# Scores of the first 128 keys in float32r halves, one tile later, in a hybrid gMLP and retention encoder step

## The chip, the cores and the metric

The kernel runs on one core of one Trainium2 chip. The metric is device time in microseconds, the median of several executions. The times before are 2776.47, 2776.78 and 2777.16 us.

## The reference

A two-layer encoder step on 256 prompt frames and 32 sample frames (288 columns in all) with a model width of 2048. Layer 0 mixes tokens by spatial gating, layer 1 by retention; each is followed by a SwiGLU feed-forward layer, and each part by a layer norm of `ALPHA * x + part(x)`. The change lies in the retention of layer 1, with 8 heads of 256 key and 512 value dimensions:

```python
def retention_block(q, k, v, s0, decay, inner, zeta, blk_decay):
    scores = jnp.einsum('bhqd,bhkd->bhqk', q, k) * decay[None]
    intra = jnp.einsum('bhqk,bhkv->bhqv', scores, v)
    cross = jnp.einsum('bhqd,bhdv->bhqv', q, s0) * inner[None, :, :, None]
    s_new = blk_decay[None, :, None, None] * s0 + jnp.einsum(
        'bhkd,bhkv->bhdv', k * zeta[None, :, :, None], v)
    return intra + cross, s_new
...
    proj = x @ w_in
    q, k, v, g = jnp.split(proj, [RET_QK, 2 * RET_QK, 2 * RET_QK + RET_V], axis=-1)
    ...
    q = rope(heads(q, RET_DK), pos) * (RET_DK ** -0.5)
    k = rope(heads(k, RET_DK), pos)
    ...
    o = (o - mu) * lax.rsqrt(var + GN_EPS)
    y = (jax.nn.silu(g.astype(jnp.float32)) * o).astype(x.dtype) @ w_out
```

All arithmetic of the reference is float32. The outputs are the encoded frames, the retention states after prompt and sample, and some rows of the gating layer.

## The kernel before

Activations lie with features on the partitions and the 288 frames as columns. A projection is a sequence of 128x128 weight blocks; a **tile** is one 128-row output, 16 blocks deep here. Precision comes from halves: `split` writes the rounded value as float32r (a cast on ACT) and the rest as a second float32r tile (a subtraction on DVE). A block then takes three float32r matmuls (weight high by x high, weight high by x low, weight low by x high; lines 106 to 108). The weights stream from HBM in chunks of eight blocks; `prep` loads chunk c + 3 and splits it into `whi` and `wlo` when chunk c begins, with three raw and four split buffers. Where the frames are 288 columns the matmul's access pattern is reordered in groups of four columns (`turned`); `fourth` does the same for the other float32r products (`mm4`, line 179).

PE runs in program order. The order of ACT, DVE and POOL is set at build time by a scheduler; each then runs its list in order. What follows a tile is put at a place in the program with `core.after(n, fn)`: `tick` is called at the end of each tile and runs what has come due.

In `retention`, the output columns come head by head: heads 0 and 1 with four gate tiles ahead of values, keys and queries; then values, keys and queries of heads 2 and 3, then both heads' gates, then half of the output projection; the same for heads 4 to 7, with the gates of 4 and 5 behind each head's queries. For each head:

- `turn` (line 705) rotates keys or queries (`rope`, six DVE operations, tiles `rk` and `rq` in the trace) when both their tiles are there. Keys go through `k_move` by a transpose and DRAM into row layout (`k_room`, `kw`), and `k_split` (line 741) makes their decayed halves, `self.wait` ticks later. Queries schedule `scores` after `self.wait` ticks. That is 3 for head 0 and 2 for the others.
- `scores` (line 761) makes three sets of float32 products into one PSUM bank: the first 128 keys by all 256 prompt queries (line 766), the second 128 keys by the second 128 queries (line 768), and the sample's keys, copied three times to 96 rows (line 713), by the sample's queries (line 770). DVE multiplies by the decay table, and the results are split for the next products.
- `v_move` and `v_split` bring the values into row layout (`v_room`, `vw`, `vz`) and split them into `vv`.
- `attend` (line 802) comes one tick after keys, values and scores are all there: products with state and values (`os`, `ss`, `ob`, `sp`), the new states written out, then `normalise` and `o_move`, which transposes the output back through DRAM (`o_room`, `of`), and `o_gate` three ticks later.

All these DRAM transfers are issued on POOL's queue. Most tiles of the stage have a single buffer.

Of the kernel before, what the change touches and what calls it, by code (L numbers as in the profile page):

```python
# [10 lines left out]
F32 = mybir.dt.float32  # L11
F32R = mybir.dt.float32r
I32 = mybir.dt.int32
AF = mybir.ActivationFunctionType
ALU = mybir.AluOpType
# [4 lines left out]
P = 128  # L20
D = 2048
KT = D // P
NP = 256
NS = 32
NT = NP + NS
# [3 lines left out]
NR = 3 * NS  # L29
# [146 lines left out]
def fourth(nc):  # L176

    def mm(out, w, x, **kw):
        nc.tensor.matmul(turned(out, 4), w, turned(x, 4), **kw)

    return mm
# [267 lines left out]
def split(nc, hi, lo, f):  # L449
    nc.scalar.copy(hi, f)  # L450
    nc.vector.tensor_tensor(lo, f, hi.bitcast(F32), ALU.subtract)  # L451
# [176 lines left out]
def retention(core, cst, x, y, lnp, prev, ins, st_p_out, st_s_out):  # L628
    tc, nc = core.tc, core.nc
    xh, xl = x  # L630
    xs = lambda k: (xh[:, k, :NT], xl[:, k, :NT])
    mm, mm4 = nc.tensor.matmul, fourth(nc)
    with ExitStack() as es:
        pool = es.enter_context(tc.tile_pool(name="ret", bufs=1, reuse_waits="tile"))
# [10 lines left out]
        nc.gpsimd.dma_start(inn, ins["inner"])  # L645
        ln = PostNorm(core, cst, x, y, lnp, 2)
        pss = pool.tile([P, 2 * NS], F32R, tag="pss", name="r_ps")
        zero = pool.tile([P, NS], F32, name="r_zero")
        nc.gpsimd.memset(zero, 0.0)
        nc.scalar.copy(pss[:NR, NS:], zero[:NR, :])  # L650
        heads = {}
# [7 lines left out]
            return t[:, :4 * NT].rearrange("p (b i s) -> p b i s", b=9, i=4)  # L659

        def rope(dst, a, b, cos, sin, nm):
            t1 = pool.tile([P, NT], F32, tag="rt1", name=f"rt1{nm}", bufs=1)
            t2 = pool.tile([P, NT], F32, tag="rt2", name=f"rt2{nm}", bufs=1)
            nc.vector.tensor_tensor(t1, a[:, :NT], cos, ALU.mult)
            nc.vector.tensor_tensor(t2, b[:, :NT], sin, ALU.mult)
            nc.vector.tensor_tensor(dst[:, 0, :NT], t1, t2, ALU.subtract)
            nc.vector.tensor_tensor(t1, a[:, :NT], sin, ALU.mult)
            nc.vector.tensor_tensor(t2, b[:, :NT], cos, ALU.mult)
            nc.vector.tensor_tensor(dst[:, 1, :NT], t1, t2, ALU.add)

        class Head:
            def __init__(self, h):
                self.h = h
                self.wait = 3 if h == 0 else 2
                self.ps = {}
                self.left = {"k", "v", "s"}
                self.open = {"o", "g"}
                self.dec = pool.tile([P, NT], F32, tag="dec", name=f"dec{h}")
                nc.gpsimd.dma_start(self.dec, ins["decay"][h])
                self.sg = pool.tile([P, 4, NT], F32, tag="rsg", name=f"rsg{h}", bufs=2)  # L680

            def evac(self, m, ps):
                h = self.h
                if m < 32:
                    self.ps[m % 2] = ps
                    if m % 2:
                        turn = lambda p=dict(self.ps): self.turn(m, p)
                        if h == 0:
                            core.after(2, turn)
                        else:  # L690
                            turn()
                elif m < 64:
                    i = m % 4
                    if i == 0:
                        self.tv = blocks(f"tv{h}", h)
                    nc.vector.transpose(self.tv[:, :, i, :], ps[:, :NT])
                    if i == 3:
                        self.v_move()
                else:
                    i = m % 4  # L700
                    nc.scalar.activation(self.sg[:, i, :], ps[:, :NT], AF.Silu)
                    if i == 3:
                        core.after(1, lambda: self.o_gate("g"))

            def turn(self, m, ps):
                h = self.h
                isk = m >= 16
                nm = ("k" if isk else "q") + str(h)
                r = pool.tile([P, 2, NP + (NR if isk else NS)], F32, tag="kr" if isk else "qr", name="r" + nm)
                rope(r, ps[0], ps[1], cs[:, 0, :], cs[:, 1, :], nm)  # L710
                if isk:
                    self.kr = r
                    nc.scalar.copy(r[:, :, NT:].rearrange("p d (r n) -> p d r n", r=2),
                                   r[:, :, NP:NT].unsqueeze(2).broadcast_to([P, 2, 2, NS]))
                    self.k_move()
                else:
                    self.qr = r
                    qf = pool.tile([P, 2, NS], F32, tag="qf", name=f"qf{h}")
                    qi = pool.tile([P, 160], F32R, tag="qi", name=f"qi{h}")
                    self.qi = qi[:, 20:20 + 4 * NS].rearrange("p (d a n) -> p d a n", d=2, a=2)  # L720
                    nc.vector.tensor_tensor(qf, r[:, :, NP:], inn[:, h, :].unsqueeze(1).broadcast_to([P, 2, NS]), ALU.mult)
                    split(nc, self.qi[:, :, 0, :], self.qi[:, :, 1, :], qf)
                    core.after(self.wait, self.scores)

            def proceed(self, what, i=3):
# [35 lines left out]
            def scores(self):  # L761
                h = self.h
                self.proceed("s")
                b = core.bank(f"sc{h}")
                for d in range(2):
                    mm(b[:, 0:NP], self.kr[:, d, 0:P], self.qr[:, d, 0:NP], start=d == 0, stop=d == 1)
                for d in range(2):
                    mm(b[:, NP:NP + P], self.kr[:, d, P:NP], self.qr[:, d, P:NP], start=d == 0, stop=d == 1)
                for d in range(2):
                    mm(b[:NR, 384:384 + NS], self.kr[:, d, NP:], self.qr[:, d, NP:], start=d == 0, stop=d == 1)  # L770
                pf = pool.tile([P, 384], F32, tag="pf", name=f"pf{h}")
                self.ph = pool.tile([P, 384], F32R, tag="ph", name=f"ph{h}")
                self.pl = pool.tile([P, 384], F32R, tag="pl", name=f"pl{h}")
                psf = pool.tile([P, NS], F32, tag="psf", name=f"psf{h}")
                nc.vector.tensor_tensor(pf[:, :NP], b[:, :NP], self.dec[:, :NP], ALU.mult)
                nc.vector.tensor_tensor(pf[:, NP:], b[:, NP:384], self.dec[:, :P], ALU.mult)
                nc.vector.tensor_tensor(psf[:NR, :], b[:NR, 384:384 + NS], self.dec[:NR, NP:], ALU.mult)
                r = slice(2 * NS, NR)
                nc.scalar.copy(pss[:NR, :NS], psf[:NR, :])
                nc.vector.tensor_tensor(pss[r, :NS], psf[r, :], pss[r, :NS].bitcast(F32), ALU.subtract)  # L780
                split(nc, self.ph, self.pl, pf)

            def v_move(self):
                h = self.h
# [135 lines left out]
        for grp in range(2):  # L920
            a, b, c, d = order[4 * grp:4 * grp + 4]
# [12 lines left out]
def hybrid_step(ctx, tc, ins, outs):  # L934
# [34 lines left out]
    ln = gmlp(core, cst, x, y, lnp, ins, outs["v"], lambda s: load(s + 4))  # L969
    ln = ffn(core, cst, x, y, lnp, 0, ln)  # L970
    ln = retention(core, cst, x, y, lnp, ln, ins, outs["st_p"], outs["st_s"])
    ffn(core, cst, x, y, lnp, 1, ln, outs["yT"])
    core.flush()
# [86 lines left out]
```

## Time and profile before

| what | value |
|---|---|
| median of the runs | 2776.78 us |
| profiled execution | 2779.29 us, its span 2777.5 us |
| granted TensorE clock | 0.999 |
| PE, DVE, ACT, POOL busy | 100%, 60%, 45%, 5% |
| retention stage | from about 1114 to 1862 us of the span |

The profile shows one execution. Busy time of PE counts each matmul with its fill and drain, so neighbouring matmuls overlap in it; the chain of waits counts from start to start. An idle engine that is not the bound costs nothing. In the trace a float32 matmul of the source stands as two rows, since it is run in two passes.

### The profile page before, as it was taken

To read this page: it belongs to the slowest core of one execution; us is meant where nothing else is said; L and a number is where in the kernel's file an instruction comes from. 1 tells how busy PE (TensorE), PEld (TensorE's weight loads), DVE (VectorE), ACT (ScalarE), POOL (GpSimd) and SP (SyncE) were. 2 spreads that over 40 slices of the span, in tenths; PEclk is the share of its full clock that TensorE was granted. 3 is DMA by queue.
4 is the path that set the end of the run, shared out by engine and by line. 5 is a ranking of instruction groups with operands and counts; after the bars stand their busy time and mean duration, and the time that the engine had idled before them with its cause. 6 is when DMAs were issued, how large, how long until landed. Compare 5 with 4: busy or idle time off the path is not lost.

```text
span 2777.5 us, 51381 instructions
## 1 busy us (share of the span) xinstructions
PE 2764.5 (100%) x21574; PEld 2750.9 (99%) x21574; DVE 1665.4 (60%) x2358; ACT 1241.7 (45%) x1645; POOL 141.3 (5%) x241
## 2 busy tenths in 40 slices
PE   9999999999999999999999999999999999999998
PEld 9999999999999999999999999999999999999998
DVE  5688854445444466767765666767844445444465
ACT  5465643433334344644543444445633433333343
POOL 1100000000000000012200111200000000000001
PEclk9999999999999999999999999999999999999999
DMA  7655455555555555567765666755555555555553
GB/s 270 217 189 166 166 178 175 172 172 174 175 175 175 172 175 178 189 205 236 230 198 173 200 216 214 232 194 175 168 174 174 175 174 173 172 173 175 175 174 126
DMA packets 147672, 515.49 MB, mean 186 GB/s; under 512 B 18080, under 2 KB 22448, under 8 KB 147408
## 3 DMA queue, kind: packets, MB, share of 16 engines
q1 hardware_dynamic: 133072, 473.47, 51.1%
q0 software_dynamic: 14224, 38.59, 4.7%
q8 instruction: 168, 2.75, 0.4%
q14 instruction: 64, 0.52, 0.0%
q10 hardware_dynamic: 144, 0.15, 0.0%
HBM read 486.98 MB, written 25.17 MB: 184 GB/s over the span
## 4 chain that ended last, share of the span: by engine, by line
PE 98%; DVE 1%; DMA 1%; issue 0%; ACT 0%; POOL 0%; SPq 0%; DVEq 0%; POOLq 0%
PE af_in L107 13%; PE af_in L108 13%; PE af_in L106 13%; PE ab_in L106 7%; PE ab_in L107 7%; PE ab_in L108 7%; PE af_out L106 6%; PE af_out L107 6%; PE af_out L108 6%; PE ab_out L107 2%; PE ab_out L106 2%; PE ab_out L108 2%; PE aa_in L108 2%; PE aa_in L106 2%; PE aa_in L107 2%; PE aa_out L106 1%
## 5 line engine op out<-in xcount | busy, mean ns | idle before, releaser
L451 DVE TENSOR_TENSOR wlo<-raw,whi 128x1024 fp32r<-128x1024 f32 (+1 forms) x892 | 1086.0, 1218 | 883.6 <-ACT whi L450 879.4
L450 ACT CAST whi<-raw 128x1024 fp32r<-128x1024 f32 (+1 forms) x892 | 933.1, 1047 | 1382.8 <-issue 336.5
L107 PE MATMUL af_in<-xl,whi 128*128 128x288 f32 (+1 forms) x2816 | 812.6, 289 | 0.0
L106 PE MATMUL af_in<-xh,whi 128*128 128x288 f32 (+1 forms) x2816 | 812.3, 288 | 0.0
L108 PE MATMUL af_in<-xh,wlo 128*128 128x288 f32 (+1 forms) x2816 | 812.3, 288 | 0.0
L108 PEld LDWEIGHTS af_in<-xh,wlo 128*128 128x128 f32 x2816 | 527.7, 187 | 0.0
L107 PEld LDWEIGHTS af_in<-xl,whi 128*128 128x128 f32 x2816 | 527.7, 187 | 0.0
L106 PEld LDWEIGHTS af_in<-xh,whi 128*128 128x128 f32 x2816 | 527.7, 187 | 0.0
L106 PE MATMUL ab_in<-xh,whi 128*128 128x288 f32 (+1 forms) x1536 | 443.9, 289 | 0.0
L107 PE MATMUL ab_in<-xl,whi 128*128 128x288 f32 (+1 forms) x1536 | 443.3, 289 | 0.0
L108 PE MATMUL ab_in<-xh,wlo 128*128 128x288 f32 (+1 forms) x1536 | 443.2, 289 | 0.0
L108 PE MATMUL af_out<-hh,wlo 128*128 128x288 f32 x1408 | 405.9, 288 | 0.0
L106 PE MATMUL af_out<-hh,whi 128*128 128x288 f32 x1408 | 405.9, 288 | 0.0
L107 PE MATMUL af_out<-hl,whi 128*128 128x288 f32 x1408 | 405.9, 288 | 0.0
L107 PEld LDWEIGHTS ab_in<-xl,whi 128*128 128x128 f32 x1536 | 287.9, 187 | 0.3
L106 PEld LDWEIGHTS ab_in<-xh,whi 128*128 128x128 f32 x1536 | 287.9, 187 | 0.3
L108 PEld LDWEIGHTS ab_in<-xh,wlo 128*128 128x128 f32 x1536 | 287.9, 187 | 0.0
L107 PEld LDWEIGHTS af_out<-hl,whi 128*128 128x128 f32 x1408 | 263.8, 187 | 0.0
L108 PEld LDWEIGHTS af_out<-hh,wlo 128*128 128x128 f32 x1408 | 263.8, 187 | 0.0
L106 PEld LDWEIGHTS af_out<-hh,whi 128*128 128x128 f32 x1408 | 263.8, 187 | 0.0
L108 PE MATMUL aa_in<-xh,wlo 128*128 128x288 f32 x512 | 148.4, 290 | 1.2 <-DVE wlo L451 1.2
L106 PE MATMUL aa_in<-xh,whi 128*128 128x288 f32 x512 | 148.7, 290 | 0.1
(240 smaller groups left out, 2867.0 us busy)
## 6 DMA issues: line engine op xcount, KB each, us to landing
raw<-in_wpack_dram SPq DMA_DIRECT2D x887, 512.0 KB, 3.3
v_room<-tv POOLq DMA_DIRECT2D x32, 144.0 KB, 5.0
of<-o_room POOLq DMA_DIRECT2D x32, 144.0 KB, 5.3
vw<-v_room POOLq DMA_DIRECT2D x8, 512.0 KB, 5.3
out_st_s_dram<-sso POOLq DMA_DIRECT2D x16, 256.0 KB, 2.6
out_st_p_dram<-so POOLq DMA_DIRECT2D x16, 256.0 KB, 2.9
o_room<-to POOLq DMA_DIRECT2D x8, 512.0 KB, 3.8
y<-in_xT_dram SPq DMA_DIRECT2D x8, 288.0 KB, 5.5
```

Source lines behind the costliest of these rows:

```text
L106: mm(ps, hi, xh, start=first, stop=False)
L107: mm(ps, hi, xl, start=False, stop=False)
L108: mm(ps, lo, xh, start=False, stop=last)
L450: nc.scalar.copy(hi, f)
L451: nc.vector.tensor_tensor(lo, f, hi.bitcast(F32), ALU.subtract)
```

## The change

The product of the first 128 keys with the 256 prompt queries is no longer two float32 matmuls but six float32r matmuls on split keys and queries. `turn` makes the halves (`qa`, `qb`, `ka`, `kb`). The sample's keys are no longer copied to 96 rows: their product has 32 rows, and the decayed sample scores are copied into the three row groups afterwards. The decayed scores are split in two pieces (256 and 128 columns). Every head waits 3 ticks, for `scores` and for `k_split` alike. Scratch tiles (`rt1`, `rt2`, `qf`, `pf`, `psf`, the zero tile) come from the norm's six shared temporary buffers (`prev.tmp`) rather than from own ones.

```diff
-        zero = pool.tile([P, NS], F32, name="r_zero")
+        zero = prev.tmp("r_zero")[:, :NS]
...
-            t1 = pool.tile([P, NT], F32, tag="rt1", name=f"rt1{nm}", bufs=1)
-            t2 = pool.tile([P, NT], F32, tag="rt2", name=f"rt2{nm}", bufs=1)
+            t1 = prev.tmp(f"rt1{nm}")
+            t2 = prev.tmp(f"rt2{nm}")
...
-                self.wait = 3 if h == 0 else 2
+                self.wait = 3
...
-                r = pool.tile([P, 2, NP + (NR if isk else NS)], F32, tag="kr" if isk else "qr", name="r" + nm)
+                r = pool.tile([P, 2, NT], F32, tag="kr" if isk else "qr", name="r" + nm)
+                parts = [pool.tile([P, 2, P if isk else NP], F32R, tag=nm[0] + x, name=nm + x) for x in "ab"]
                 rope(r, ps[0], ps[1], cs[:, 0, :], cs[:, 1, :], nm)
                 if isk:
                     self.kr = r
-                    nc.scalar.copy(r[:, :, NT:].rearrange("p d (r n) -> p d r n", r=2),
-                                   r[:, :, NP:NT].unsqueeze(2).broadcast_to([P, 2, 2, NS]))
                     self.k_move()
+                    self.kp = parts
+                    split(nc, *parts, r[:, :, :P])
                 else:
...
+                    self.qp = parts
+                    split(nc, *parts, r[:, :, :NP])
                     core.after(self.wait, self.scores)
...
-                for d in range(2):
-                    mm(b[:, 0:NP], self.kr[:, d, 0:P], self.qr[:, d, 0:NP], start=d == 0, stop=d == 1)
+                (kh, kl), (qh, ql) = self.kp, self.qp
+                prods = [(l[:, d, :], r[:, d, :]) for d in range(2) for l, r in ((kh, qh), (kh, ql), (kl, qh))]
+                for i, (l, r) in enumerate(prods):
+                    mm4(b[:, 0:NP], l, r, start=i == 0, stop=i == len(prods) - 1)
...
-                    mm(b[:NR, 384:384 + NS], self.kr[:, d, NP:], self.qr[:, d, NP:], start=d == 0, stop=d == 1)
-                pf = pool.tile([P, 384], F32, tag="pf", name=f"pf{h}")
+                    mm(b[:NS, 384:384 + NS], self.kr[:, d, NP:], self.qr[:, d, NP:], start=d == 0, stop=d == 1)
+                pf = [prev.tmp(f"pf{h}{i}") for i in range(2)]
...
-                nc.vector.tensor_tensor(psf[:NR, :], b[:NR, 384:384 + NS], self.dec[:NR, NP:], ALU.mult)
-                r = slice(2 * NS, NR)
-                nc.scalar.copy(pss[:NR, :NS], psf[:NR, :])
-                nc.vector.tensor_tensor(pss[r, :NS], psf[r, :], pss[r, :NS].bitcast(F32), ALU.subtract)
-                split(nc, self.ph, self.pl, pf)
+                nc.vector.tensor_tensor(psf[:NS, :], b[:NS, 384:384 + NS], self.dec[:NS, NP:], ALU.mult)
+                for r in range(2):
+                    nc.scalar.copy(pss[r * NS:(r + 1) * NS, :NS], psf[:NS, :])
+                nc.vector.tensor_tensor(pss[2 * NS:NR, :NS], psf[:NS, :], pss[:NS, :NS].bitcast(F32), ALU.subtract)
+                split(nc, self.ph[:, :NP], self.pl[:, :NP], pf[0][:, :NP])
+                split(nc, self.ph[:, NP:], self.pl[:, NP:], pf[1][:, :P])
```

More of the change, by code (lines that the diff above doesn't have):

```diff
@@ L712, in turn @@
                     self.kr = r
-                    nc.scalar.copy(r[:, :, NT:].rearrange("p d (r n) -> p d r n", r=2),
-                                   r[:, :, NP:NT].unsqueeze(2).broadcast_to([P, 2, 2, NS]))
                     self.k_move()
+                    self.kp = parts
+                    split(nc, *parts, r[:, :, :P])
                 else:
                     self.qr = r
-                    qf = pool.tile([P, 2, NS], F32, tag="qf", name=f"qf{h}")
+                    qf = prev.tmp(f"qf{h}")[:, :2 * NS].rearrange("p (d n) -> p d n", d=2)
                     qi = pool.tile([P, 160], F32R, tag="qi", name=f"qi{h}")
@@ L769, in scores @@
                 for d in range(2):
-                    mm(b[:NR, 384:384 + NS], self.kr[:, d, NP:], self.qr[:, d, NP:], start=d == 0, stop=d == 1)
-                pf = pool.tile([P, 384], F32, tag="pf", name=f"pf{h}")
+                    mm(b[:NS, 384:384 + NS], self.kr[:, d, NP:], self.qr[:, d, NP:], start=d == 0, stop=d == 1)
+                pf = [prev.tmp(f"pf{h}{i}") for i in range(2)]
                 self.ph = pool.tile([P, 384], F32R, tag="ph", name=f"ph{h}")
                 self.pl = pool.tile([P, 384], F32R, tag="pl", name=f"pl{h}")
-                psf = pool.tile([P, NS], F32, tag="psf", name=f"psf{h}")
-                nc.vector.tensor_tensor(pf[:, :NP], b[:, :NP], self.dec[:, :NP], ALU.mult)
-                nc.vector.tensor_tensor(pf[:, NP:], b[:, NP:384], self.dec[:, :P], ALU.mult)
-                nc.vector.tensor_tensor(psf[:NR, :], b[:NR, 384:384 + NS], self.dec[:NR, NP:], ALU.mult)
-                r = slice(2 * NS, NR)
-                nc.scalar.copy(pss[:NR, :NS], psf[:NR, :])
-                nc.vector.tensor_tensor(pss[r, :NS], psf[r, :], pss[r, :NS].bitcast(F32), ALU.subtract)
-                split(nc, self.ph, self.pl, pf)
+                psf = prev.tmp(f"psf{h}")[:, :NS]
+                nc.vector.tensor_tensor(pf[0][:, :NP], b[:, :NP], self.dec[:, :NP], ALU.mult)
+                nc.vector.tensor_tensor(pf[1][:, :P], b[:, NP:384], self.dec[:, :P], ALU.mult)
+                nc.vector.tensor_tensor(psf[:NS, :], b[:NS, 384:384 + NS], self.dec[:NS, NP:], ALU.mult)
[4 more added lines that the diff above has]
+                split(nc, self.ph[:, NP:], self.pl[:, NP:], pf[1][:, :P])
             def v_move(self):
```

## The prediction

> **What bounds the kernel now.** I read the page first, then busy time by stage, the chain of waits around one head's scores, the groups of instructions of the retention stage, and last the timelines of POOL, DVE and ACT around the hand-over from head 1 to head 2.
>
> ```profile
> span 2777.5 us, 51381 instructions
> PE 2764.5 (100%) x21574; PEld 2750.9 (99%) x21574; DVE 1665.4 (60%) x2358; ACT 1241.7 (45%) x1645; POOL 141.3 (5%) x241
> PE 98%; DVE 1%; DMA 1%; issue 0%; ACT 0%; POOL 0%; SPq 0%; DVEq 0%; POOLq 0%
> ```
>
> The chain that ended last is PE for 98% of the span. A matmul's duration here includes its fill and drain, so a busy PE alone proves little; the chain does, since it counts start to start. Two stretches, an undisturbed piece of the output projection and the whole retention stage:
>
> ```profile
> 1490.00:1540.00 50.00, 50.00 (x397) 50.00 (x396) 26.94 (x33) 17.95 (x17) 0.00 (x0) 1.00 0.52 173
> 1113.80:1862.00 748.20, 748.20 (x5722) 738.02 (x5721) 512.50 (x819) 354.98 (x474) 112.01 (x191) 1.00 0.65 209
> ```
>
> In the retention stage (second row) DVE works 512 of 748 us and ACT 355, at a granted clock of 1.00. PE sets the pace, at 50/397 = 0.126 us for a 288-column float32r matmul (first row). So only two things can move the time: fewer PE microseconds, or a helper so late that PE waits.
>
> The chain around the scores and the attention step of head 1 (start, length, what):
>
> ```profile
> 1120.06 0.53 PE m L304 x4
> ...
> 1275.09 0.86 PE sc L766 x4
> 1275.95 0.45 PE sc L768 x4
> 1276.39 0.28 PE sc L770 x4
> ...
> 1282.86 1.12 PE os L179 x5
> 1283.98 0.45 PE ss L179 x2
> 1284.43 1.99 PE ob L179 x9
> 1286.41 2.65 PE sp L179 x12
> ```
>
> Each float32 matmul of the source runs as two passes, so L766's two matmuls are four rows of 0.215 us. The 512-column float32r products (sp) cost 2.65/12 = 0.221 us each. Between os at 1282.86 and the end of sp at 1289.06 lie 6.2 us; from the scores' end (1276.67) to os is one projection tile, 6.2 us.
>
> **The change, part by part.**
>
> *Scores of the first 128 keys (L766).* Four float32 passes over 256 columns become six float32r passes over 256 columns (two halves of the key dimension, three products each). Their price is not in the trace. The line through 288 columns at 0.126 and 512 at 0.221 has a slope of 0.424 ns a column, so 256 columns cost about 0.112 us, and six cost 0.675. Below that it can hardly go: 256 times the bare slope is 0.109, six of them 0.65. Above, the slowest float32r row of this kind is L304, 288 columns without the four-column reordering, at 0.53/4 = 0.1325, six of them 0.795. The new products use the reordering of the sp group, so I take 0.675: 0.86 - 0.675 = 0.185 us less for each head, with 0.065 and 0.21 as bounds.
>
> [...]
>
> *Scores of the sample keys (L770).* The stationary side shrinks from 96 to 32 columns (the key copies are gone); 32 columns still stream. The loads, from the instructions of L768 and L770:
>
> ```profile
> L768 PEld LDWEIGHTS sc<-rq,rk x32: 190/191/192, 1212.9 to 1809.9; 128*128 128x128 f32 x32
> L770 PEld LDWEIGHTS sc<-rq,rk x32: 163/165/165, 1213.5 to 1810.3; 128*96 128x96 f32 x32
> ```
>
> From 256 columns (0.215 a pass) to 128 (0.45/4 = 0.112), streaming costs 0.80 ns a column, so 32 columns alone would be about 0.035 a pass, 0.14 for four. They take 0.28: here the load is what lasts, and a load gets 26 ns shorter for 32 columns less. The new set lies between 0.14 (the load no longer shows) and 0.28 (nothing gained). 64 columns less take away 52 ns a pass by the load rows, more than the 35 ns that stand above streaming, so I take 0.14: 0.14 less a head.
>
> L768 is unchanged. Sum for PE: 8 x (0.185 + 0.14) = 2.6 us less; bounds 8 x 0.065 = 0.5 and 8 x (0.21 + 0.14) = 2.8.
>
> *New work on ACT and DVE.* Rotated keys (256 columns) and queries (512) are split into halves, the decayed scores in two pieces instead of one, the sample scores copied twice at 32 partitions; the copy at L713 goes. The nearest groups:
>
> ```profile
> L450 ACT CAST r_oh<-rsg 128x288 fp32r<-128x288 f32 x28 | 10.0, 429 | 1.6 <-DVE rsg L890 1.6
> L450 ACT CAST vv<-vz 32x512 fp32r<-32x512 f32 x8 | 4.9, 614 | 0.3 <-DMA vz<-v_room 0.3
> L713 ACT COPY rk<-rk 128x128 f32<-128x128 f32 x8 | 2.3, 292 | 1.3 <-DVE rk L669 1.3
> L779 ACT CAST r_ps<-psf 96x32 fp32r<-96x32 f32 x8 | 1.7, 213 | 0.0
> L451 DVE TENSOR_TENSOR r_ol<-rsg,r_oh 128x288 fp32r<-128x288 f32 x28 | 10.9, 451 | 0.0
> L451 DVE TENSOR_TENSOR vv<-vz,vv 32x512 fp32r<-32x512 f32 x8 | 5.4, 681 | 0.2
> L450 ACT CAST whi<-raw 128x1024 fp32r<-128x1024 f32 x233 | 245.4, 1053 | 351.0 <-PE ab_in L107 228.9 <-PE ab_out L107 61.8 <-issue 29.4
> L451 DVE TENSOR_TENSOR wlo<-raw,whi 128x1024 fp32r<-128x1024 f32 x233 | 284.3, 1220 | 167.5 <-ACT whi L450 166.0
> ```
>
> ACT: about 0.4 + 0.6 + 0.2 + 0.2 - 0.3 = 1.1 us more a head; DVE: 0.4 + 0.7 + 0.2 = 1.3. Times eight that is 9 and 10 us in a stage with 393 and 236 us of idle time, so I cost it at nothing. What hides it is the lead of the weight splits: of the 351 us that ACT idles before casting weights, 291 end with a matmul that gives a buffer back, so ACT is ahead and waits for PE. The code prepares a chunk of eight blocks when the third one before it begins. A chunk lasts 24 x 0.126 = 3.0 us; three of them less 1.05 + 1.22 of splitting leave 6.8 us by which the helpers may be late. If that cover is gone, each microsecond beyond it is a microsecond of PE.
>
> *One tile later.* Scores and decayed keys (L741, L723) move by 6.1 us, and the attention step, which waits for both, with them: state copies, transposes and its ten DMAs on POOL's queue too. The order of PE instructions changes, their number only by the passes above. Around the scores of head 1:
>
> ```profile
> 1272.03 0.46 DVE L669 TENSOR_TENSOR rq<-rt1q,rt2q 128x288 f32<-128x288 f32 x1
> ...
> 1274.18 1.13 DVE L752 SCALAR_TENSOR_TENSOR kl<-kw,r_zt,kh 128x128 fp32r<-128x128 f32 x4
> ```
>
> The rotated query is done at 1272.5 and the scores start at 1275.09: 2.6 us, short for a cast of 0.6 and a subtraction of 0.7 behind other work, and PE, which runs in program order, would hold every later projection behind them. With the extra tile it is 8.7 us, so PE does not wait for the halves. The decayed keys move with the attention step that reads them, at the same distance. Heads 3 and 7 have eight gate tiles before the output projection; their attention output needs four to five tiles and stays in time. The next head's decay load waits for the score products and so comes 6 us later, with seven or more tiles left until its use.
>
> *Temporaries.* The rotation's scratch, the decayed scores and the zero tile move into the six shared temporary buffers. The first are written and read by DVE within a tile: nothing. The zero tile is held long:
>
> ```profile
> L649 POOL MEMSET r_zero<- x1: 147/147/147, 983.3 to 983.3; 128x32 f32 x1
> L650 ACT CAST r_ps<-r_zero x1: 201/201/201, 1115.6 to 1115.6; 96x32 fp32r<-96x32 f32 x1
> ```
>
> If it takes one of the six at 983 and returns it at 1116, the norm of the first feed-forward layer has five for its squares; each is used within a microsecond or two, so again nothing.
>
> **Sum.** The profiled execution took 2779.29 us (span 2777.5 and 1.8 around it); 2.6 less is 2776.7. The median of the runs shown lies 2.5 below that execution, so by the same difference I forecast 2776.78 - 2.6 = 2774.2. That is 0.09%, under the 0.2% (5.6 us) that a measurement of this kernel can tell from no change.
>
> **The rivals.**
>
> *A queue on POOL blocks ACT (slower).* Where a head's values follow directly on the head before (1 to 2, 2 to 3, 6 to 7), the move brings the two heads' transfers together; from the timelines of DVE, POOL and ACT:
>
> ```profile
> 1301.27 0.48 DVE L696 STREAM_TRANSPOSE tv<-ab_in 128x288 f32<-128x288 f32 x1 [0.81 <-PE ab_in L108]
> ```
> ```profile
> 1297.39 0.74 POOL L879 DMA_DIRECT2D o_room<-to  x1 [1.18 <-DVE to L876]
> 1301.81 2.48 POOL L882 DMA_DIRECT2D of<-o_room  x4 [3.68 <-issue]
> 1304.28 2.41 POOL L459 DMA_DIRECT2D v_room<-tv  x4
> 1313.62 0.75 POOL L460 DMA_DIRECT2D vw<-v_room  x1 [6.93 <-DMA v_room<-tv]
> ```
> ```profile
> 1318.67 1.05 ACT L450 CAST vv<-vw 128x1024 fp32r<-128x1024 f32 x1 [0.51 <-DMA vw<-v_room]
> ```
>
> The values are transposed at 1301.75, but v_room goes out only at 1304.28, behind of. ACT's cast then waits for vw: already just in time. Moved by 5.8 us, o_room goes out near 1303.2 and of near 1307.6. If v_room stays behind of, vw and the cast come 5.8 us later, with ACT's weight casts queued behind that cast and DVE's subtractions behind ACT. Put end to end, the wait (5.8), the value casts (1.05 + two of 0.61), the value subtractions (1.2 + 0.7) and the new splits (1.2) make 11.2, which is 4.4 beyond the cover of 6.8; three places give 13.2, less 2.6: about 2787. It decides once helpers are blocked for over 6.8 us; a loss above 8.2 us in all makes the kernel slower by more than 0.2%. Against it: v_room is ready (1301.75) before o_room would be (1303.2), so a queue ordered by readiness lets it pass, and vw comes earlier than now.
>
> [...]
>
> *The same in small.* One or two of the places lose 1 to 3 us each, as when only part of that burst falls together: 2775 to 2779, still within 0.2%.
>
> *The new products are no cheaper.* If each waited for its own weight load of 0.19 us (the L768 row), six would take 1.15 instead of 0.86: 8 x (0.29 - 0.14) = 1.2 more, 2778.0. Against: projections load the same 128 columns for every matmul and still run at 0.126.
>
> [...]
>
> *Faster by over 0.2%.* The rewritten passes cost 8 x (0.86 + 0.28) = 9.1 us in all; 5.6 would mean that over 60% of them vanish, or a shorter wait elsewhere that the chain does not show.
>
> **How the numbers follow.** Forecast (0.5 to 2.8 us less, no new wait): 0.66. Small waits: 0.10. Products no cheaper: 0.04. These three are the 0.80 for within 0.2%. POOL's queue, slower: 0.16. Faster: 0.04. The range holds the first three and leaves out the last two, 0.20: from 2773.4 (2.8 less, and 0.6 for the spread between runs) to 2779.5 (the small waits, and the same spread).
>
> **What would show it right or wrong.** In the changed profile: six passes of 0.11 us in place of four of 0.215, the L770 set near 0.14, PE still 98% of the chain, and ACT's weight casts still ended by PE giving buffers back. POOL's order around 1304 tells whether v_room passes of. The forecast is wrong if wlo or whi appear as releasers of ab_in matmuls between 1280 and 1330, 1340 and 1385 or 1765 and 1810, or if the six passes take over 0.86.

## The result and the profile after

The changed kernel takes 2795.11 us (median; 2794.29 to 2796.98), the kernel before 2776.91 on the same chip: 18.2 us longer, a ratio of 1.0063 [1.0053, 1.0073]. The forecast was 2774.2, with a range from 2773.4 to 2779.5. Single executions of several kernels here, the one before included, run some 36 us longer than the rest; where one stands among a run's executions its interval is wide, and the median is the better figure. The profiled execution took 2794.63 us. Its page:

```profile
span 2792.9 us, 51454 instructions
PE 2781.2 (100%) x21590; PEld 2768.1 (99%) x21590; DVE 1673.5 (60%) x2382; ACT 1247.2 (45%) x1669; POOL 141.2 (5%) x241
PE 99%; DVE 0%; issue 0%; ACT 0%; DVEq 0%; POOL 0%; POOLq 0%
```

Nothing here looks like a new wait. PE carries 99% of the chain, and there are 16 more passes than before, two a head, as the diff says. The busy sums can't show what happened, because PE counts as busy either way. What shows it is the number of matmuls in windows of equal length. First the kernel before, then after (window, length, then busy time and count of PE, PEld, DVE, ACT and POOL, granted clock, DMA share, GB/s):

```profile
1300.00:1320.00 20.00, 20.00 (x160) 20.00 (x159) 14.54 (x23) 9.38 (x13) 7.52 (x13) 1.00 0.89 281
1440.00:1490.00 50.00, 50.00 (x397) 50.00 (x396) 30.37 (x38) 18.23 (x20) 0.00 (x0) 1.00 0.52 174
```
```profile
1240.00:1260.00 20.00, 20.00 (x160) 20.00 (x159) 15.05 (x23) 10.16 (x14) 5.35 (x10) 1.00 0.84 261
1300.00:1320.00 20.00, 20.00 (x152) 20.00 (x152) 13.98 (x22) 7.93 (x11) 8.85 (x15) 1.00 0.92 264
1440.00:1490.00 50.00, 50.00 (x377) 50.00 (x376) 28.54 (x35) 17.69 (x21) 0.00 (x0) 1.00 0.50 168
1710.00:1730.00 20.00, 20.00 (x152) 20.00 (x151) 11.46 (x14) 8.40 (x11) 2.47 (x4) 1.00 0.74 222
1850.00:1870.00 20.00, 20.00 (x153) 20.00 (x151) 10.38 (x12) 8.62 (x14) 2.69 (x5) 1.00 0.70 215
1910.00:1960.00 50.00, 50.00 (x397) 50.00 (x396) 41.62 (x71) 26.53 (x39) 0.00 (x0) 1.00 0.52 170
```

50 us hold 377 projection matmuls or 397 of them, 0.133 us each or 0.126, at a granted clock of 1.00, and the weight loads keep step. These are the same instructions on the same tiles: the change doesn't touch them. The windows show only these two paces. By the starts of single matmuls the slow one holds from the end of the attention step of heads 1, 3, 5 and 7 to the next head's scores (for head 7, to the norm behind the stage): 1292 to 1337, 1407 to 1606, 1700 to 1771 and 1841 to 1905 us. That is 378 us, and 5% of it is 18.9 us. One group of 256 matmuls, first after (within 1407 to 1607), then before (1407 to 1590), shows its whole mean moved, with no idle time in front (0.0):

```profile
L106 PE MATMUL ab_out<-r_oh,whi 128*128 128x288 f32 x256 | 75.8, 296 | 0.0
```
```profile
L106 PE MATMUL ab_out<-r_oh,whi 128*128 128x288 f32 x256 | 73.8, 288 | 0.0
```

The mean of one (296 ns, with its fill and drain) is 8 ns above that of before (288), near the 6.7 ns by which their starts lie further apart.

The chain around head 1's scores and attention step:

```profile
1278.32 0.68 PE sc L179 x6
1279.00 0.45 PE sc L773 x4
1279.44 0.24 PE sc L775 x4
1279.68 0.33 PE ab_in L106
...
1285.98 1.12 PE os L179 x5
1287.10 0.48 PE ss L179 x2
1287.58 2.00 PE ob L179 x9
1289.58 2.67 PE sp L179 x12
```

The six passes take 0.68, as forecast. The sample's set takes 0.24 and the first projection matmul behind it 0.33; before, these two were 0.28 and 0.21. From the scores' start to the second projection matmul it was 1.80 us (0.86 + 0.45 + 0.28 + 0.21) and is 1.70 now: 8 x 0.10 = 0.8 us gained. In the attention step ss, ob and sp are a little longer (0.48, 2.00, 2.67 for 0.45, 1.99, 2.65). Four such steps cost 0.2 us by single starts (6.27 for 6.21 each). So 18.9 + 0.2 - 0.8 = 18.3 us, against 18.2 measured by the medians.

### The profile page after: what moved, and what is told of

Its sections match the earlier page's. It is cut to its first block, busy times and chain, and to the rows that moved or that the text cites. A ratio compares the mean times of both kernels' runs of the same rounds, so it can differ in the third digit from the quotient of the medians.

```text
span 2792.9 us, 51454 instructions
## 1 busy us (share of the span) xinstructions
PE 2781.2 (100%) x21590; PEld 2768.1 (99%) x21590; DVE 1673.5 (60%) x2382; ACT 1247.2 (45%) x1669; POOL 141.2 (5%) x241
## 4 chain that ended last, share of the span: by engine, by line
PE 99%; DVE 0%; issue 0%; ACT 0%; DVEq 0%; POOL 0%; POOLq 0%
PE af_in L108 13%; PE af_in L106 13%; PE af_in L107 13%; PE ab_in L106 7%; PE ab_in L107 7%; PE ab_in L108 7%; PE af_out L107 6%; PE af_out L108 6%; PE af_out L106 6%; PE ab_out L106 2%; PE ab_out L108 2%; PE ab_out L107 2%; PE aa_in L108 2%; PE aa_in L107 2%; PE aa_in L106 2%; PE aa_out L106 1%
## 5 line engine op out<-in xcount | busy, mean ns | idle before, releaser
L106 PE MATMUL ab_out<-r_oh,whi 128*128 128x288 f32 x512 | 150.2, 293 | 0.0
L107 PE MATMUL ab_out<-r_ol,whi 128*128 128x288 f32 x512 | 150.2, 293 | 0.0
```

Source lines behind the costliest of these rows:

```text
L106: mm(ps, hi, xh, start=first, stop=False)
L107: mm(ps, hi, xl, start=False, stop=False)
```

## The experiments

The question was what in the change sets the pace of matmuls that it doesn't touch. Each diff below is against the changed kernel unless it says otherwise; a line in parentheses stands for the code that it names, and `...` for code left out.

**The wide set back.** The sample's keys are copied to 96 columns again, into a shared temporary; the six passes stay.

```
+  (a copy of r[:, :, NP:NT], three times, into kx)
-  mm(b[:NS, 384:384 + NS], self.kr[:, d, NP:], ...)
+  mm(b[:NR, 384:384 + NS], self.kx[:, d, :], ...)
```

> The changed kernel, but the sample keys are again copied to 96 columns (in a temporary), so their product loads 96 columns and the decayed sample scores are handled as before; the six float32r products, the wait of 3 and the shared temporaries stay. Theory N (the narrow 32-column set leaves the matmul stream in a rhythm that turns slow, 0.133 us a projection matmul instead of 0.127, after the attention step of every second head): no slow stretches, about 1.4 us under before, 2775.5. Rival S (the six float32r products do it): slow stretches stay, about 2794 to 2796. Rival W (the later place of scores and attention does it): slow stretches stay, 2794 to 2796.

Measured: 2802.23 us, ratio 1.0092 [1.0076, 1.0109]. Slow behind every head from 1 to 7. A window of it:

```profile
1360.00:1380.00 20.00, 20.00 (x152) 20.00 (x151) 11.45 (x16) 7.39 (x9) 7.77 (x13) 1.00 0.94 268
```

So the narrow set alone isn't to blame: without it more heads are slow.

**The float32 products back.** The first 128 keys are scored in float32 as before; the narrow set, the later place and the temporaries stay.

```
-  for i, (l, r) in enumerate(prods):
-      mm4(b[:, 0:NP], l, r, ...)
+  for d in range(2):
+      mm(b[:, 0:NP], self.kr[:, d, 0:P], self.qr[:, d, 0:NP], ...)
```

> The changed kernel, but the first 128 keys are multiplied in float32 again, without the halves of keys and queries; the narrow sample set, the wait of 3 and the temporaries stay. Theory N: slow stretches stay, some 380 us at 5% more, about 2796 to 2798. Rival S: none, about 2777.5. Rival W: slow stretches stay, about 2796 to 2798.

Measured: 2808.24 us, 1.0114 [1.0099, 1.0129]. Slow behind all eight heads, head 0's too:

```profile
1240.00:1260.00 20.00, 20.00 (x152) 20.00 (x151) 13.02 (x19) 9.99 (x14) 3.68 (x6) 1.00 0.82 237
```

Either half of the change to the products is enough alone, and worse than both together. The losses don't add, so they aren't costs of the instructions. What does add up is time at the slow pace. By single starts it is 378 us in the changed kernel, 538 with the wide set and 594 here; 5% of that is 18.9, 26.9 and 29.7 us, and the three kernels are 18.2, 25.6 and 31.6 us longer than the one before. What the scores themselves gain or lose (0.8 and 1.5 gained, 0.6 lost) and the longer attention steps (0.2 to 0.5) are most of the rest.

**The later place alone.** The kernel before, with three ticks for every head.

```
-  self.wait = 3 if h == 0 else 2
+  self.wait = 3
```

> The kernel before with nothing changed but the wait: 3 ticks for every head. Theory N and rival S: as before, 2776.9 within 0.5. Rival W: slow stretches appear, 2790 or more.

Measured: 2776.95 us, 0.9999 [0.9990, 1.0008]. The window that is slow in the changed kernel holds 160:

```profile
1300.00:1320.00 20.00, 20.00 (x160) 20.00 (x159) 14.91 (x21) 8.51 (x12) 9.51 (x16) 1.00 0.93 276
```

**The same products in another order.** The sample's set first, then the six, then the second 128 keys. The instructions are the same ones, and ACT, DVE, POOL and SP run the same lists in the same order.

```
+  (the two narrow products of L775)
   (the six products)
   (the two products of L773)
-  (the two narrow products of L775)
```

> The changed kernel with the same products in another order: the narrow sample set first, then the six float32r products, the float32 set of the second 128 keys last. Theory N, where it is the way in which the scores end that sets the rhythm: no slow stretches, about 2775 to 2776. If N holds wherever the narrow set stands: slow stretches, 2790 or more. Rival W: 2794 to 2796.

Measured: 2776.10 us, 0.9997 [0.9987, 1.0006]. No slow stretch is left; a window inside what was the longest one:

```profile
1450.00:1470.00 20.00, 20.00 (x160) 20.00 (x159) 11.91 (x17) 7.20 (x7) 0.00 (x0) 1.00 0.52 165
```

An order alone takes away 19 us. It also clears the rest of the change: halves, shared temporaries and the later place are all in this kernel, and it is no slower than before. The forecast saving isn't there either (2776.10 for 2776.60), and the chain shows where part of it went:

```profile
1278.58 0.24 PE sc L769 x4
1278.82 0.88 PE sc L179 x6
1279.70 0.45 PE sc L775 x4
```

Behind the narrow set the six take 0.88 instead of 0.68: the 0.20 us that the matmul behind this set takes above its 0.13 in the changed kernel (0.33) fall on the six here.

**Is it the last set that decides?** That was my reading of the order. The narrow set goes between the six and the second 128 keys, which again come last.

```
   (the six products)
+  (the two narrow products)
   (the two products of the second 128 keys)
-  (the two narrow products)
```

> The changed kernel with the narrow sample set between the six float32r products and the float32 set of the second 128 keys, which now comes last. Theory P (the way the scores end leaves the stream of matmuls in one of two rhythms that look alike until the attention step, and one of them comes out of it at 0.133 us): ending on the 128-column set, no slow stretches, about 2776. Rival O (what matters is that the narrow set stands first): slow stretches stay, 2790 or more.

Measured: 2795.60 us, 1.0064 [1.0026, 1.0103]. Slow behind the odd heads as in the changed kernel:

```profile
1300.00:1320.00 20.00, 20.00 (x152) 20.00 (x152) 13.44 (x28) 8.31 (x9) 6.30 (x11) 1.00 0.84 265
```

My reading fell. The second 128 keys come last here and in the order before this one, and only one of the two is slow.

**A product behind the attention step.** If the pace is a state of PE's stream, something odd in the stream should end it. One product of 288 columns, whose result nobody reads, behind each head's attention products:

```
+  mm(core.bank(f"kick{h}")[:, :NT], cst["one_r"], xh[:, 0, :NT], start=True, stop=True)
```

> The changed kernel with one more product of 288 columns per head right behind the attention step's products, whose result nobody reads. Theory P: the slow rhythm is a state of the stream that any odd product can end, so the 0.133 us stretches are gone or cut to a few us; 8 x 0.13 us more work, about 2777 to 2778. Rival A (the slow pace comes from where operands lie or from what ACT, DVE and the DMAs do after an attention step): stretches stay, 2796.

Measured: median 2778.07 us, the kernel before 2777.26 beside it (0.9985 [0.9953, 1.0018]). Two windows of its profile:

```profile
400.00:450.00 50.00, 50.00 (x377) 50.00 (x376) 22.25 (x23) 19.32 (x24) 0.00 (x0) 1.00 0.51 169
1480.00:1500.00 20.00, 20.00 (x160) 20.00 (x159) 11.61 (x15) 6.57 (x7) 0.00 (x0) 1.00 0.51 167
```

The second row is the retention stage: the slow stretches are gone, for eight products of about 0.13 us. The first row is a surprise. The profiled execution took 2813.27 us, 35 above the median, and in it the slow pace held from 326 to 1055 us, in a stage that no kernel here changes; 729 us x 5% is 36. So the pace can be taken up without any of these products.

**The 96-column set first.** The sample's keys are copied to 96 columns as in the kernel before, and their set stands first; the six passes follow, and the float32 set of the second 128 keys comes last.

```
+  (the two 96-column products, on copied keys)
   (the six products)
   (the two products of the second 128 keys)
-  (the two narrow products)
```

> Six float32r products, but the sample keys copied to 96 columns as before and their set put first, the 128-column float32 set last. Theory P: no slow stretches; the scores cost 1.5 us a head as in the first experiment instead of 1.69 before, so 8 x 0.19 = 1.5 us under before: 2775.1. Rival (any float32r scores upset the rhythm unless the narrow set stands first): slow stretches, 2795 or more.

Measured: median 2779.05 us, before 2777.26 (0.9984 [0.9951, 1.0017]).

```profile
1240.00:1260.00 20.00, 20.00 (x152) 20.00 (x152) 11.46 (x15) 7.82 (x11) 6.15 (x10) 1.00 0.81 242
1300.00:1320.00 20.00, 20.00 (x161) 20.00 (x160) 14.45 (x29) 8.36 (x9) 6.85 (x12) 1.00 0.87 267
```

Only head 0 turned slow: 58 us, 3 us lost. The expected gain was missed by that.

**64 columns.** The sample's keys copied twice.

```
+  (a copy of r[:, :, NP:NT], twice, into kx)
-  mm(b[:NS, 384:384 + NS], self.kr[:, d, NP:], ...)
+  mm(b[:2 * NS, 384:384 + NS], self.kx[:, d, :], ...)
```

> The changed kernel, order of the sets as there, with the sample keys copied to 64 columns for their product; the decayed scores are taken from the first 32 rows as in the change. If only the 32-column load cannot be pulled ahead of the matmul in front of it, the gap of 0.205 us ahead of the set is gone and its four passes cost about 0.055 us each, some 0.15 us a head less than with 32 columns. If the gap stays, no change. Slow stretches may be there or not: both theories leave it open, since the scores' length changes.

Measured: 2795.80 us, 1.0068 [1.0021, 1.0115], slow where the changed kernel is.

```profile
1338.82 0.35 PE sc L778 x4
1339.17 0.33 PE ab_in L106
```

The set and the matmul behind it take 0.68, 0.11 more than with 32 columns: the gap stays (at head 1 no load is under way from 1279.80 to 1279.92), and the four passes take 0.35 for 0.24.

**Where the state is set.** Four more kernels place the odd product. The first is the 96-column order with the product behind head 0's attention step alone.

```
+  if h == 0: mm(core.bank(f"kick{h}")[:, :NT], cst["one_r"], xh[:, 0, :NT], ...)
```

> The kernel with the 96-column sample set first, six float32r products next and the 128-column float32 set last, and one extra 288-column product, whose result nobody reads, behind the attention step of head 0 alone: the only head after which that kernel fell into the slow rhythm. Theory P: the slow stretch after head 0 is gone, 3 us less than without the extra product; 1.4 us under before, 2775.5. Rival: the extra product moves the later heads into the slow rhythm, 2790 or more.

Measured: median 2778.12 us, before 2776.75 (1.0008 [0.9979, 1.0038]). Head 0's stretch is gone, and head 1 has turned slow in its place:

```profile
1240.00:1260.00 20.00, 20.00 (x160) 20.00 (x159) 13.29 (x21) 10.23 (x16) 3.68 (x6) 1.00 0.80 242
1300.00:1320.00 20.00, 20.00 (x152) 20.00 (x152) 13.98 (x21) 8.19 (x12) 8.64 (x14) 1.00 0.90 260
```

Head 1's own instructions are the same in both kernels, so a head's pace depends on what the stream did a head earlier. The second is the changed kernel, with the product *ahead* of every attention step: behind the scores and the projection tile that follows them.

```
+  mm(core.bank(f"kick{h}")[:, :NT], cst["one_r"], xh[:, 0, :NT], ...)   # first of attend's products
```

> The changed kernel with the extra product ahead of every attention step instead of behind it. If the state is set by the scores and carried through the tiles between (theory P), the extra product resets it: every attention step takes 6.22 us rather than 6.33 in half of the heads, no slow stretches, about 2777 to 2778. If the attention step itself makes it (rival), half of the heads still come out slow: 2796.

Measured: 2777.04 us, before 2776.75 (1.0002 [0.9993, 1.0011]).

```profile
1450.00:1470.00 20.00, 20.00 (x160) 20.00 (x159) 12.96 (x17) 6.57 (x7) 0.00 (x0) 1.00 0.54 181
```

No slow stretch, and all attention steps at their short length (6.20 to 6.21; the expectation's 6.22 and 6.33 are 6.21 and 6.27 from start to start). This speaks for the reading that the scores leave something behind; that it passes through a whole tile of projections that run at the usual 0.126; and that the attention step turns it into the slow pace, unless a product in between clears it.

The length of the scores bears this out. From their start to the second projection matmul they take 1.693 us ahead of each slow stretch of the changed kernel and 1.697 to 1.701 ahead of the others. With the product ahead of the attention steps, heads 1 to 7 all have 1.693 to 1.694, and none turns slow.

The last two put the 96-column order and that product ahead of the attention step of head 0 alone, and of heads 0 and 1.

```
+  if h < 1:   # and, in the second kernel, h < 2
+      mm(core.bank(f"kick{h}")[:, :NT], cst["one_r"], xh[:, 0, :NT], ...)
```

> The 96-column sample set first, six float32r products, the 128-column float32 set last, and the extra product ahead of head 0's attention step alone. Theory P: head 0 leaves its attention step fast; the later heads were fast when they came out of a fast or slow stretch by themselves in one run and not in another, so head 1 may still turn slow. All fast: 1.3 us under before, 2775.4; head 1 slow for 46 us: 2777.8.

> The same with the extra product ahead of the attention steps of heads 0 and 1. Theory P: both leave it fast, no slow stretch at all, 1.2 us under before: 2775.5. Rival (resetting two heads only hands the slow rhythm on to head 2): 2778 or more.

Measured: 2775.74 us (0.9994 [0.9985, 1.0003]) and 2775.56 us (0.9995 [0.9987, 1.0004]), before 2776.68. Neither profile has a slow stretch in the retention stage. The second one's chain at head 2's scores:

```profile
1335.13 0.28 PE sc L772 x4
1335.41 0.76 PE sc L179 x6
1336.17 0.45 PE sc L778 x4
1336.62 0.13 PE ab_in L106
```

From the scores' start to the second projection matmul it is 1.62 us for 1.80 before; eight times 0.18 less two products of 0.13 is 1.2, and the medians give 1.1. This is the best version: some 19 us under the changed kernel. Whether it beats the kernel before isn't settled, since the interval holds 1.

## Why the prediction was wrong

*The step that failed* is the sentence "So only two things can move the time: fewer PE microseconds, or a helper so late that PE waits". It took 0.126 us for granted as the price of every unchanged matmul. A third thing can move the time: the same matmuls at 0.133. This is worth seven times the whole forecast saving, and no rival held it. That the change gives a slower kernel had 0.16, for another mechanism, which didn't come. By the prediction's own list of signs (wlo or whi as releasers, six passes over 0.86) the forecast would have stood: the list looked for waits and for the price of new products only. Nor would 2774.2 have come without the slow pace: the first two terms together made 0.8 us less in the chain rather than 2.6, and the reordered kernel, which has no slow stretch, is 0.5 us under the one before.

*First term, right.* Six passes at 0.68 for 0.675.

*Second term, of the wrong sign.* The set and the matmul behind it were to lose 0.14 us and gained 0.08 (0.24 + 0.33 for 0.28 + 0.21). The line of load times was read as if a narrow load were a wide one made shorter. The timeline of weight loads shows another thing (start, length, tile):

```profile
1278.84 0.41 PEld L773 LDWEIGHTS sc<-rq,rk 128*128 128x128 f32 x3
1279.37 0.20 PEld L775 LDWEIGHTS sc<-rq,rk 128*32 128x32 f32 x4
1279.61 0.19 PEld L106 LDWEIGHTS ab_in<-xh,whi 128*128 128x128 f32 x1
```
```profile
1275.57 0.63 PEld L768 LDWEIGHTS sc<-rq,rk 128*128 128x128 f32 x4
1276.12 0.44 PEld L770 LDWEIGHTS sc<-rq,rk 128*96 128x96 f32 x4
```

Before (second fence) the first 96-column load starts at 1276.12, while the last load of the 128 columns still runs (to 1276.20). After, no load is under way from 1279.25 to 1279.37: PE doesn't fetch the narrow weights ahead here. The float32 set of 64 columns has the same gap of 0.12 us, that of 96 none. The attention step has none either, though its first product (os, float32r) loads 64 columns behind loads of 128: it starts 0.13 us after the last projection matmul. So a narrower load alone makes no gap, and what does isn't shown.

*New work on ACT and DVE, right.* The new casts and subtractions cost what was estimated, and the weight splits stay ahead: the groups, and ACT's waits from 1407 to 1607 (us in total, times, longest):

```profile
L450 ACT CAST q1a<-rq 128x512 fp32r<-128x512 f32 x1 | 0.6, 621 | 0.0
L451 DVE TENSOR_TENSOR q1b<-rq,q1a 128x512 fp32r<-128x512 f32 x1 | 0.7, 685 | 0.0
```
```profile
ACT whi L450 <- PE ab_out L107: 67.3, 32, 2.2
ACT whi L450 <- PE ab_in L107: 47.6, 23, 2.5
```

ACT still waits for PE to give buffers back, in the slow stretches too.

*POOL's queue, nearly as late as feared and harmless.* The timeline of POOL at the hand-over from head 1 to head 2:

```profile
1299.47 0.67 POOL L459 DMA_DIRECT2D v_room<-tv  x1
...
1301.36 1.25 POOL L459 DMA_DIRECT2D v_room<-tv  x2
1306.25 2.40 POOL L888 DMA_DIRECT2D of<-o_room  x4 [3.64 <-DMA o_room<-to]
1308.64 0.61 POOL L459 DMA_DIRECT2D v_room<-tv  x1
1316.52 0.75 POOL L460 DMA_DIRECT2D vw<-v_room  x1
```

Three of v_room's four transfers go ahead of `of`, the last behind it. In time of the span vw comes 2.9 us later than before (1313.62). But the values are transposed earlier here, at 1298.68 for 1301.27, so counted from there vw is 5.5 us later, close to the 5.8 of the rival. What didn't come is the block of ACT:

```profile
1320.99 1.05 ACT L450 CAST whi<-raw 128x1024 fp32r<-128x1024 f32 x1 [1.70 <-issue]
1321.94 1.04 ACT L450 CAST vv<-vw 128x1024 fp32r<-128x1024 f32 x1
```

The cast of vw follows a weight cast without a wait, and no wait of PE is listed in the whole stage.

*One tile later and the temporaries, right:* the run with the wait alone gives 2776.95, and the reordered one with everything in it 2776.10.

*The evidence of L304.* The prediction took L304's 0.1325 as the price of a product without the reordering. The reordered projections also run at 0.133 in a slow stretch, so that row alone doesn't prove a price of the order. The traces lean the prediction's way, though: in all fourteen profiles the 144 projection matmuls around L304 (1113.6 to 1133.1 us before) that aren't reordered either run at 0.133 on average, between reordered ones at 0.127 on either side. That reordered products run at 0.126 outside the slow stretches stands.

*What is open.* What inside PE holds the state. The clock (1.00 in every window shown), the operands (the same rows at both paces), the helpers and the DMA traffic are excluded as far as these traces show: the reordered kernel gives all other engines the same lists, and the kernel with the product behind every attention step took 2778 us in most executions and 2813 in the one seen to run slow. Which run of products leaves the state couldn't be reduced to a rule: neither the narrow set, nor the six passes, nor the last set decides alone.

## What to carry to other kernels

PE was 100% busy and carried 98% of the chain before and 99% after, so neither figure told the pace of 0.133 from that of 0.126. Compare the number of matmuls in equal windows of the two profiles before anything else. Here the order of the scores' 14 passes a head decided whether the unchanged matmuls of 378 us (some 2800, as estimated from 378 us at 0.133) were slow: 2795.11 us or 2776.10. So try a few odd products between long runs in two or three orders, or put one spare product behind them (2778.07 us), before judging their price; its place matters, since behind one attention step alone it only moved the slow stretch to the next head. A float32 set of 32 or 64 columns started 0.205 us after the start of the last pass of the 128-column set in front of it, one of 96 columns 0.111.

## What the hardware showed that was not expected

The same float32r matmuls of 288 columns run back to back at either 126.7 or 133.3 ns by their starts, with the clock at 1.00 (from 1440 to 1490 us before and after), and keep the pace for up to hundreds of microseconds (the slow one from 1407 to 1606 after). As an estimate from starts: 512 columns are 220 ns apart in the attention step, so a column costs (220 - 126.7) / 224 = 0.417 ns and 288 columns 120; what stands above that is 6.7 ns at the one pace and 13.3, twice as much, at the other. The slow pace appears by itself too: from 326 to 1055 us in one profiled execution, and from 6 to 140 us in two others (that of the narrow set in the middle, and that of the product ahead of head 0 alone), which took some 5 us more than their medians. The change from 128 to 32 float32 columns, and that to 64, took 0.205 us from pass to pass, where the 128-column passes are 0.112 apart.
